# Layer 0's last group of the down product by seven products, its quarters folded as they finish

## The chip, the cores and the metric

One core of one Trainium2 chip runs the whole program. The metric is the time of one execution on the device, in microseconds (us), median of several runs.

## What is computed

Two layers on x of 512 tokens by 1024 features, all in float32. The reference, cut to what matters here:

```python
for layer in range(2):
    h = rms_norm(x, g_mix[layer])
    x = x + (even_mixer if layer == 0 else odd_mixer)(h, ...)     # projections, attention, output product
    h = rms_norm(x, g_mlp[layer])
    x = x + squared_relu_mlp(h, w_up[layer], w_down[layer])

def squared_relu_mlp(h, w_up, w_down):
    u = einsum("bsd,df->bsf", h, w_up)                  # 512 x 1024 by 1024 x 4096
    return einsum("bsf,fd->bsd", square(relu(u)), w_down)   # 512 x 4096 by 4096 x 1024
```

`rms_norm` divides a token's row by the root of its mean square and multiplies it by a gain per feature.

## The kernel before

Every float32 product is made of three products of a rounded high part and the low rest (`whi`, `wlo` of a weight; likewise of the data): high by high, low by high, high by low, added in one PSUM bank. A weight arrives by DMA as `wraw` or `mraw`; ScalarE (ACT) or GpSimd (POOL) copies the high part, VectorE (DVE) or POOL subtracts it for the low one. TensorE is PE in the profile, the DMA queue SP.

The function `mlp` makes a layer's second half out of a list of items. An item ("U", u) makes 256 of the 4096 hidden features in four steps of twelve matmuls (`up`). A down group collects four U items, 1024 hidden features. Three of layer 0's groups, and all four of layer 1's, are items ("T", g): a block scheme in which seven products take the place of eight. The table `ORDER` lists the seven (which weights, which data, which bank pair X, Y or Z), 28 steps of six matmuls; `combine_t` adds a finished bank, scaled per token by `r2col`, to one of four quarters `rest[e, t]` (feature half e, token half t). Sums of weight blocks are made on DVE by `sums_t`. With product 2 the scheme starts two banks of Y by one small product each (`L990`).

The last group of layer 0 is different: four items ("E", 3, dp), 16 steps of twelve matmuls (`direct`), each dp giving 256 features in the transposed layout that the next layer wants. For it the data of the U items 12 to 15 are scaled beforehand by a broadcast of the tokens' mean squares (`ssum`, the product of `L826`). The three T groups' quarters are turned by `fold` (four transposes and an add per 128 features) into the residual `back`, which comes back from `xmid`, while U 14 runs. `direct_end` then finishes 128 features at a time: add, high part `hn` on ACT, low on DVE, square on ACT, sum of squares on DVE.

Layer 1 begins with `vf_c`: `project` of 272 columns (values and forget gates), eight weights of 128x272 (k = 0 to 7, a step of 128 features each), twelve matmuls per weight into `pj0` to `pj3` (a bank for 128 tokens each). After a few of them (`STATS`) the caller runs `stats()`: `token_sums` on PE (`pc`) and `col_stats` on DVE, a chain of small instructions from `msv` to `rcol`. Then `use` needs `rcol`: `fz` on DVE, the four transposes `pz` on PE, the values `v` on ACT and DVE. `qk_c(0)` follows, 512 columns, in the same four banks; its eight tiles are split by `PAT_ATT`, that is, highs on POOL, lows by turns on DVE and POOL.

The order of each engine's instructions is set when the program is built; the engines work through theirs in order. Steps are counted in `mlp`'s main loop: weights are split six steps ahead (`R`), loads are issued two steps before that (`LS`), and `at(n, f)` puts an extra piece of work behind step n.

## Time and profile before

| | us |
|---|---|
| median of 3 runs (1156.47 to 1157.99) | 1157.99 |
| the profiled execution | 1157.34 |
| its span, first to last instruction | 1155.2 |
| PE busy | 1140.4 (99%) |
| DVE busy | 862.1 (75%) |
| ACT busy | 649.2 (56%) |
| POOL busy | 197.5 (17%) |
| mean granted clock of PE | 0.998 |

The span is the part that the trace covers; the time of the same execution is 2.1 us longer. A row of the timeline has the start from the span's first instruction, the length, the engine, the line of the code and what is written and read; `x8` counts instructions that were merged. Matmul rows overlap, since they are pipelined: their spacing tells the pace, not their length.

### The profile page before, as it was taken

Reading aid. Unit: us, or ns where it says so; the run is one execution under the profiler, and the core shown is the slowest. Engines: PE = TensorE matmul, PEld = TensorE weight load, DVE = VectorE, ACT = ScalarE, POOL = GpSimd, SP = SyncE. Lnnn points to the kernel's source line nnn. Section 1 sums busy time; section 2 is a strip of 40 time slices with the busy share of each in tenths; the row PEclk is TensorE's granted clock in tenths of the full one; section 3 lists DMA queues with packets and bytes.
Section 4 is the critical chain, followed back from the end, with each engine's and each line's share of the span. In section 5 each row is a group of like instructions: output and inputs, shape, how many; then the busy total and the mean of one; then the engine's idle time right before and its main releaser. Section 6 shows DMA issues by size and latency. Waiting matters only on the chain.

```text
span 1155.2 us, 16365 instructions
## 1 busy us (share of the span) xinstructions
PE 1140.4 (99%) x5758; PEld 956.8 (83%) x5758; DVE 862.1 (75%) x1791; ACT 649.2 (56%) x1344; POOL 197.5 (17%) x292
## 2 busy tenths in 40 slices
PE   9999999999999999999999999999999999999998
PEld 7987887888888888888988888888888888888887
DVE  7878999967857858755647877878848759669586
ACT  7555867656656455444326675665656455465452
POOL 0445524100000000000345545432000000000000
PEclk9999999999999999999999999999999999999999
DMA  8432114530531630723543333344420722523403
GB/s 289 132 92 74 40 54 146 200 129 37 185 107 37 219 110 4 250 72 105 154 123 108 103 106 99 106 128 128 164 74 25 231 73 70 186 73 115 150 28 110
DMA packets 91329, 133.83 MB, mean 116 GB/s; under 512 B 6112, under 2 KB 54240, under 8 KB 91248
## 3 DMA queue, kind: packets, MB, share of 16 engines
q1 hardware_dynamic: 90208, 130.63, 35.5%
q10 hardware_dynamic: 1040, 2.16, 0.5%
q8 instruction: 45, 0.74, 0.3%
q14 instruction: 36, 0.29, 0.1%
HBM read 119.63 MB, written 6.32 MB: 109 GB/s over the span
## 4 chain that ended last, share of the span: by engine, by line
PE 86%; DVE 6%; DMA 2%; ACT 2%; issue 2%; POOL 1%; SPq 0%; DVEq 0%; POOLq 0%; ACTq 0%
PE up L166 10%; PE up L170 10%; PE up L169 10%; PE pj L235 4%; PE pj L237 4%; PE pj L236 4%; PE Y L999 3%; PE Y L998 3%; PE Y L996 3%; PE O L406 3%; PE PT L386 2%; PE Z L999 2%; PE X L998 2%; PE Z L998 2%; PE X L999 2%; PE X L996 2%
## 5 line engine op out<-in xcount | busy, mean ns | idle before, releaser
L166 PE MATMUL up<-xin,whi 128*128 128x512 f32 x512 | 200.8, 392 | 0.0
L794 ACT CAST whi<-wraw 128x512 fp32r<-128x512 f32 x228 | 139.3, 620 | 107.5 <-PE up L170 47.8
L170 PE MATMUL up<-xin,whi 128*128 128x512 f32 x512 | 199.4, 389 | 0.0
L169 PE MATMUL up<-xin,wlo 128*128 128x512 f32 x512 | 199.2, 389 | 0.0
L795 DVE TENSOR_TENSOR wlo<-wraw,whi 128x512 fp32r<-128x512 f32 x228 | 150.6, 686 | 61.2 <-ACT whi L794 60.6
L154 POOL TENSOR_SCALAR whi<-wraw 128x512 fp32r<-128x512 f32 x88 | 58.2, 663 | 462.3 <-PE pj L237 419.8
L170 PEld LDWEIGHTS up<-xin,whi 128*128 128x128 f32 x512 | 96.1, 188 | 20.1
L169 PEld LDWEIGHTS up<-xin,wlo 128*128 128x128 f32 x512 | 96.2, 188 | 19.8 <-issue 0.2
L166 PEld LDWEIGHTS up<-xin,whi 128*128 128x128 f32 x512 | 96.1, 188 | 19.8 <-issue 0.2
L794 ACT CAST whi<-mraw 128x512 fp32r<-128x512 f32 x112 | 68.0, 620 | 53.1 <-DVE mraw L894 22.5
L366 ACT ACTIVATE P<-P,negm 128x128 f32<-128x128 f32 (+5 forms) x128 | 69.4, 543 | 41.9 <-DVE negm L363 39.4
L943 ACT ACTIVATE u<-up 128x512 f32<-128x512 f32 x64 | 38.3, 599 | 91.8 <-PE up L170 91.8
L235 PE MATMUL pj<-whi,hn 128*128 128x512 f32 (+2 forms) x256 | 88.7, 346 | 0.0
L237 PE MATMUL pj<-whi,hn 128*128 128x512 f32 (+2 forms) x256 | 86.9, 339 | 0.0
L236 PE MATMUL pj<-wlo,hn 128*128 128x512 f32 (+2 forms) x256 | 86.8, 339 | 0.0
L795 DVE TENSOR_TENSOR wlo<-mraw,whi 128x512 fp32r<-128x512 f32 x112 | 74.5, 683 | 6.5 <-ACT whi L794 6.4
L815 DVE TENSOR_TENSOR t<-u 128x256 f32<-128x256 f32 x56 | 23.2, 423 | 68.1 <-ACT u L1076 66.2
L157 POOL TENSOR_TENSOR wlo<-wraw,whi 128x512 fp32r<-128x512 f32 x48 | 64.3, 1341 | 21.2 <-ACT whi L152 18.7
L996 PE MATMUL Y<-whi,t 128*128 128x512 f32 x168 | 65.4, 389 | 0.0
L998 PE MATMUL Y<-wlo,t 128*128 128x512 f32 x168 | 65.4, 389 | 0.0
L999 PE MATMUL Y<-whi,t 128*128 128x512 f32 x168 | 65.4, 389 | 0.0
L374 POOL TENSOR_SCALAR P<-P,rden 128x256 f32<-128x256 f32 (+2 forms) x96 | 48.5, 508 | 83.2 <-DVE rden L369 77.7
(213 smaller groups left out, 2788.4 us busy)
## 6 DMA issues: line engine op xcount, KB each, us to landing
wraw<-in_w_up SPq DMA_DIRECT2D x64, 512.0 KB, 4.5
wraw<-in_w_down SPq DMA_DIRECT2D x50, 512.0 KB, 4.1
mraw<-in_w_down SPq DMA_DIRECT2D x28, 512.0 KB, 4.8
wraw<-in_w_in_odd SPq DMA_DIRECT2D x22, 512.0 KB, 3.6
wraw<-in_w_in_even SPq DMA_DIRECT2D x17, 512.0 KB, 4.9
K<-K SPq DMA_DIRECT2D x26, 256.0 KB, 2.9
bias<-csp SPq DMA_DIRECT2D x16, 256.0 KB, 3.3
wraw<-in_w_out_odd SPq DMA_DIRECT2D x8, 512.0 KB, 3.6
```

Of the source, the lines that this page charges most:

```text
L166: m = nc.tensor.matmul(o, wh, xh, start=start, stop=False, skip_group_check=more)
L169: nc.tensor.matmul(o, wl, xh, start=False, stop=False, skip_group_check=more)
L170: nc.tensor.matmul(o, wh, xl, start=False, stop=stop, skip_group_check=more)
L235: nc.tensor.matmul(o, xh, hi[:, :n], start=k == 0, stop=False)
L236: nc.tensor.matmul(o, xh, lo[:, :n], start=False, stop=False)
L237: nc.tensor.matmul(o, xl, hi[:, :n], start=False, stop=k == DC - 1)
L366: nc.scalar.activation(p[:, :ne], p[:, :ne], AF.Exp, scale=-1.0, bias=negm[:, i:i + 1], accum_out=den[:, i:i + 1])
L794: sca(nc.scalar.copy(dst_h, src))
L795: late.append(lambda: vec(nc.vector.tensor_sub(dst_l, src, dst_h.bitcast(F32))))
L996: m = nc.tensor.matmul(o, sh, hi, start=new and k == 0, stop=False, skip_group_check=not new)
L998: nc.tensor.matmul(o, sh, lo, start=False, stop=False, skip_group_check=not new)
L999: nc.tensor.matmul(o, sl, hi, start=False, stop=k == 3, skip_group_check=not new)
```

## The change

Layer 0's last group becomes an item ("T", 3) as in layer 1, right behind U 15. So `direct`, `direct_end`, the data scaled beforehand and the broadcast product go. The order of the seven products changes for all eight T groups: 12 is fourth, 4 sixth (before 4 fourth, 12 sixth), and weight block 12 is loaded four steps earlier. A quarter of `rest` is folded after the product that finishes it, in halves of 256 features by 256 tokens: (0, 0) behind steps 18 and 19 of the 28, (1, 1) behind 22 and 23, (0, 1) behind 26 and 27, (1, 0) after the last. Each fold takes four transposes, one add, two highs on ACT, two lows on DVE, a square on ACT and, from the second on, a sum of squares (POOL; DVE for the last quarter). `token_sums` adds two columns of partial sums, eight products for four. `back` returns into other buffers. `qk_c(0)` is split by ACT and DVE.

```diff
-FIN12 = (0, 5)
-BACK = (0, 0, 1, 1)
-FOLD = (0, 0, 1, 1, 2, 2, 3, 3)
-STATS = 3
+BACK = (2, 2, 7, 7)
+FOLD = {(0, 0): (18, 19), (1, 1): (22, 23), (0, 1): (26, 27), (1, 0): (28, 28)}
+STATS = 5
...
-                    return project([(g * 768, g * 768 + 512)], qk_use(g, 8))
+                    return project([(g * 768, g * 768 + 512)], qk_use(g, 8), PAT_ATT if g else PAT_START)
...
         for t in range(NT):
-            m = nc.tensor.matmul(pc[:, t:t + 1], ssum[:, t * P:(t + 1) * P], ones[:, :1], start=True, stop=True)
...
+            for k, a in enumerate(parts_):
+                m = nc.tensor.matmul(pc[:, t:t + 1], a[:, t * P:(t + 1) * P], ones[:, :1], start=k == 0,
+                                     stop=k == len(parts_) - 1)
...
-                pr = bank("pB", "r2")
-                tc.keep_in_program_order(nc.tensor.matmul(pr, ones, ssum, start=True, stop=True))
-                vec(nc.vector.tensor_scalar(ssum, pr, 1.0 / D, EPS, op0=OP.mult, op1=OP.add))
...
-                if g < 3 or last:
-                    items.append(("T", g))
-                else:
-                    items += [("E", g, dp) for dp in range(4)]
+                items.append(("T", g))
...
-            LOADS = {-2: 11, -1: 21, 0: 22, 6: 12, 16: 220}
+            LOADS = {-2: 11, -1: 21, 0: 22, 2: 12, 16: 220}
...
-            ORDER = ((11, "b11", "X"), (1, "t1", "Z"), (2, "t2", "Y"), (4, "b22", "Z"), (3, "t3", "Y"), (12, "b21", "X"),
+            ORDER = ((11, "b11", "X"), (1, "t1", "Z"), (2, "t2", "Y"), (12, "b21", "X"), (3, "t3", "Y"), (4, "b22", "Z"),
                      (22, "t4", "Y"))
...
-            def direct(j, p, hi, lo):
...
-            def direct_end(j, p):
...
-            def fold(c):
-
+            def fold(e, t, half):
+
+
+                dp = 2 * e + half
...
                 pt = bank("pB", "rT")
...
+                for cc in range(2):
+                    for b in range(2):
+                        pin("p", nc.tensor.transpose(pt[:, cc * 256 + b * P:cc * 256 + (b + 1) * P],
+                                                     rest[e, t][:, b, (2 * half + cc) * P:(2 * half + cc + 1) * P], ident))
+                ts = slice(t * 256, t * 256 + 256)
+                a = back[dp][:, :, ts]
+                vec(nc.vector.tensor_add(a, pt.rearrange("p (c t) -> p c t", c=2), a))
+                for cc in range(2):
+                    h, c = hn[2 * dp + cc], 2 * dp + cc
+                    g = gcol[:, 8 * (li + 1) + c:8 * (li + 1) + c + 1]
+                    sca(nc.scalar.activation(h[:, 0, ts], a[:, cc], AF.Copy, scale=g))
+                    late.append(lambda h=h, g=g, x=a[:, cc]: vec(nc.vector.scalar_tensor_tensor(
+                        h[:, 1, ts], x, g, h[:, 0, ts].bitcast(F32), op0=OP.mult, op1=OP.subtract)))
+                ss = res["ss"][:, :, ts]
...
+                    sq = mp.tile([P, 2, 256], F32, tag="sq", bufs=2, name="sq")
+                    sca(nc.scalar.activation(sq, a, AF.Square))
+                    if (e, t) == (1, 0):
+                        late.append(lambda: vec(nc.vector.tensor_add(ss, ss, sq)))
+                    else:
+                        pool(nc.gpsimd.tensor_add(ss, ss, sq))
+                if (e, t) in ((0, 1), (1, 0)):
+                    nc.scalar.dma_start(xsp[dp], back[dp])
...
-            return hn, lambda: col_stats(token_sums(res["ssum2"]))
+            return hn, lambda: col_stats(token_sums([res["ss"][:, k] for k in range(2)]))
```

What this does to the order of the instructions is seen best at layer 1's first projection. On DVE before, around the statistics (`msv`, `ecol`, `rsqb`, `rsq`, up to `rcol`); `wlo` of 128x272 is the low part of a weight of the first projection, of 128x512 one of the second:

```order
L967 SCALAR_TENSOR_TENSOR hn<-back,gcol,hn 128x512
L615 TENSOR_TENSOR ssum_5510<-ssum_5510,sqx 128x512
L157 TENSOR_TENSOR wlo<-wraw,whi 128x272
L141 TENSOR_SCALAR msv<-pc 128x4
L142 TENSOR_SCALAR ecol<-msv 128x4
L131 TENSOR_SCALAR rsqb<-msv 128x4
L132 TENSOR_SCALAR rsq<-rsqb 128x4
L157 TENSOR_TENSOR wlo<-wraw,whi 128x512
L134 SCALAR_TENSOR_TENSOR rsq<-msv,rsq 128x4
L759 MEMSET one 16x512
L135 TENSOR_TENSOR rsq<-rsq 128x4
L136 SCALAR_TENSOR_TENSOR rsq<-rsq 128x4
```

The eighth 128x272 low is the last instruction ahead of the statistics. On DVE in the changed program, from the same instruction on:

```order
L140 TENSOR_SCALAR msv<-pc 128x4
L141 TENSOR_SCALAR ecol<-msv 128x4
L130 TENSOR_SCALAR rsqb<-msv 128x4
L131 TENSOR_SCALAR rsq<-rsqb 128x4
L133 SCALAR_TENSOR_TENSOR rsq<-msv,rsq 128x4
L134 TENSOR_TENSOR rsq<-rsq 128x4
L135 SCALAR_TENSOR_TENSOR rsq<-rsq 128x4
L156 TENSOR_TENSOR wlo<-wraw,whi 128x272
L133 SCALAR_TENSOR_TENSOR rsq<-msv,rsq 128x4
L156 TENSOR_TENSOR wlo<-wraw,whi 128x272
L134 TENSOR_TENSOR rsq<-rsq 128x4
L156 TENSOR_TENSOR wlo<-wraw,whi 128x512
```

Two 128x272 lows now come behind seven and eight instructions of the statistics, and one 128x512 low less far behind them. The rows that follow there, to `rcol` and `fz`:

```order
L135 SCALAR_TENSOR_TENSOR rsq<-rsq 128x4
L760 MEMSET one 16x512
L133 SCALAR_TENSOR_TENSOR rsq<-msv,rsq 128x4
L156 TENSOR_TENSOR wlo<-wraw,whi 128x512
L134 TENSOR_TENSOR rsq<-rsq 128x4
L156 TENSOR_TENSOR wlo<-wraw,whi 128x512
L135 SCALAR_TENSOR_TENSOR rcol<-rsq 128x4
L156 TENSOR_TENSOR wlo<-wraw,whi 128x512
L746 SCALAR_TENSOR_TENSOR fz<-pj_5857,rcol,bfor 128x16
L746 SCALAR_TENSOR_TENSOR fz<-pj_5858,rcol,bfor 128x16
```

Between the last 128x272 low and `fz` stand four 128x512 lows, where before two stood in the whole chain. On PE in the changed program, around `pc` (`whi_5938` and `wlo_5939` belong to the sixth weight, `5995` and `5996` to the seventh, `5999` and `6000` to the eighth):

```order
L234 MATMUL pj3_5860<-whi_5938,hn_5732 128x272
L235 MATMUL pj3_5860<-wlo_5939,hn_5732 128x272
L621 MATMUL pc_5954<-ones_79,ss_5665 128x1 x8
L236 MATMUL pj3_5860<-whi_5938,hn_5732 128x272
L234 MATMUL pj0_5857<-whi_5995,hn_5750 128x272
L234 MATMUL pj1_5858<-whi_5995,hn_5750 128x272
L234 MATMUL pj2_5859<-whi_5995,hn_5750 128x272
L234 MATMUL pj3_5860<-whi_5995,hn_5750 128x272
L235 MATMUL pj0_5857<-wlo_5996,hn_5750 128x272
L236 MATMUL pj0_5857<-whi_5995,hn_5750 128x272
L234 MATMUL pj0_5857<-whi_5999,hn_5751 128x272
```

Before, `pc` stood behind the third weight's twelve matmuls, 36 of 96 in all; now it stands behind the sixth's but one, 71 of 96. On ACT in the changed program, from the last 128x272 highs to the values:

```order
L1044 DMA xsp<-back 128x1024
L151 CAST whi<-wraw 128x272 x2
L151 CAST whi<-wraw 128x512 x7
L160 ACTIVATE v_5853<-pj_5857,rcol 128x4x64
L160 ACTIVATE v_5853<-pj_5858,rcol 128x4x64
L753 ACTIVATE fe<-pz 16x512
```

Before, the last 128x272 high was followed at once by the four `v`; now seven 128x512 highs of the second projection stand between.

## Rows read from the trace of the kernel before

**Rows 1.** The page, part 1: busy us (share of the span) xinstructions.
```profile
PE 1140.4 (99%) x5758; PEld 956.8 (83%) x5758; DVE 862.1 (75%) x1791; ACT 649.2 (56%) x1344; POOL 197.5 (17%) x292
```

**Rows 2.** Timeline of PE, end of layer 0, layer 1's first projection: start, length, line, op.
```profile
519.85 0.39 PE L166 MATMUL dn<-s,whi 128*128 128x512 f32 x1
...
563.14 0.39 PE L170 MATMUL dn<-s,whi 128*128 128x512 f32 x1
...
563.37 0.28 PE L235 MATMUL pj<-whi,hn 128*128 128x272 f32 x1
...
567.88 0.95 PE L621 MATMUL pc<-ones,ssum 128*128 128x1 f32 x8
...
568.69 0.37 PE L235 MATMUL pj<-whi,hn 128*128 128x272 f32 x1
...
576.29 0.49 PE L749 MATMUL pz<-ident,fz 128*16 128x128 f32 x3
```

**Rows 3.** Timeline of DVE, same stretch: start, length, line, op, [idle before].
```profile
550.61 0.79 DVE L157 TENSOR_TENSOR wlo<-wraw,whi 128x272 fp32r<-128x272 f32 x2
...
568.86 0.16 DVE L141 TENSOR_SCALAR msv<-pc 128x4 f32<-128x4 f32 x1 [2.10 <-PE pc L621]
...
571.19 0.16 DVE L134 SCALAR_TENSOR_TENSOR rsq<-msv,rsq 128x4 f32<-128x4 f32 x1
...
571.39 1.15 DVE L135 TENSOR_TENSOR rsq<-rsq 128x4 f32<-128x4 f32 x1
...
574.68 0.53 DVE L745 SCALAR_TENSOR_TENSOR fz<-pj,rcol,bfor 128x16 f32<-128x16 f32 x2
...
575.45 0.48 DVE L162 SCALAR_TENSOR_TENSOR v<-pj,rcol,v 128x256 fp32r<-128x256 f32 x1 [0.23 <-ACT v L161]
```

**Rows 4.** Timeline of PE, last group of layer 1: the start-up products and the next matmul.
```profile
1115.45 0.61 PE L990 MATMUL Y<-whi,b 128*128 128x512 f32 x2
1115.90 0.39 PE L996 MATMUL X<-whi,b 128*128 128x512 f32 x1
```

**Rows 5.** Timeline of PE, mean squares of layer 0, then of layer 1.
```profile
254.70 0.95 PE L621 MATMUL pc<-ones,ssum 128*128 128x1 f32 x8
...
256.68 0.39 PE L169 MATMUL up<-xin,wlo 128*128 128x512 f32 x1
...
848.25 0.95 PE L621 MATMUL pc<-ones,ssum 128*128 128x1 f32 x8
...
849.38 0.39 PE L169 MATMUL up<-xin,wlo 128*128 128x512 f32 x1
```

**Rows 6.** Windows: length, busy PE PEld DVE ACT POOL, PEclk, DMA share, GB/s.
```profile
576.30:596.00 19.70, 19.70 (x91) 16.30 (x89) 6.24 (x12) 5.04 (x8) 10.87 (x12) 1.00 0.52 159
1112.70:1130.00 17.30, 17.30 (x78) 14.31 (x77) 15.95 (x24) 10.47 (x20) 0.00 (x0) 1.00 0.00 1
1130.00:1151.40 21.40, 21.40 (x95) 17.41 (x93) 15.39 (x24) 6.77 (x12) 0.00 (x0) 1.00 0.38 135
```

**Rows 7.** Groups of instructions by shape, 480 to 620 us: count, busy, mean ns, idle before.
```profile
L795 DVE TENSOR_TENSOR wlo<-wraw,whi 128x512 fp32r<-128x512 f32 x26 | 17.4, 686 | 6.2 <-ACT whi L794 6.1
...
L157 DVE TENSOR_TENSOR wlo<-wraw,whi 128x272 fp32r<-128x272 f32 x8 | 3.4, 436 | 0.7 <-ACT whi L152 0.7
...
L1029 DVE SCALAR_TENSOR_TENSOR rest<-Y,r2col,rest 128x512 f32<-128x512 f32 x2 | 1.4, 751 | 0.7 <-PE Y L999 0.7
...
L759 DVE MEMSET one<- 16x512 f32 x1 | 0.5, 485 | 0.0
```

**Rows 8.** The page, part 6, loads of layer 1's projection: KB each, us to landing.
```profile
wraw<-in_w_in_odd SPq DMA_DIRECT2D x22, 512.0 KB, 3.6
```

**Rows 9.** Timeline of POOL beside those DVE rows.
```profile
571.23 1.29 POOL L157 TENSOR_TENSOR wlo<-wraw,whi 128x512 fp32r<-128x512 f32 x1
```

**Rows 10.** Windows in layer 0, columns as above: PE busy, then PEclk.
```profile
99.80:103.56 3.76, 2.06 (x10) 1.09 (x9) 2.29 (x3) 0.12 (x1) 3.53 (x3) 1.00 0.74 211
103.56:106.98 3.42, 3.42 (x12) 2.84 (x11) 2.02 (x3) 1.04 (x2) 1.31 (x2) 0.50 0.00 0
```

More of the change, by code (lines that the diff above doesn't have):

```diff
@@ L1076, in square @@
                         sca(nc.scalar.activation(v[:, e], v[:, e], AF.Square))
-                def whole(e):
-                    s = slot("s") if u < 15 else mp.tile([P, 2, 512], F32R, tag="t24", bufs=2, name="s")
-                    halves(s[:, 0], s[:, 1], v[:, e])
-                    store[u, e] = s
-                def part(e):
-                    sca(nc.scalar.activation(v[:, e], v[:, e], AF.Square))
-                    vec(nc.vector.tensor_mul(v[:, e], v[:, e], ssum))
-                    whole(e)
-                    if u == 15:
-                        catch_up()
-                if not last and u >= 12:
-                    return [lambda: part(0), lambda: part(1)]
                 def tsum():
@@ L1106, in t_part @@
                 def t_part(i):
-                    if i and u % 4 == 0 and u:
+                    if i and (u % 4 == 0 and u or u == 15 and not last):
                         s = mp.tile([P, 2, 512], F32R, tag="t24", bufs=2, name="t24")
@@ L1129, in plan @@
                 n0 = first[j + 1]
-                if not last and u >= 12:
-                    offs = FIN12 if u == 12 else (0, 1)
-                else:
-                    offs = FIN15 if u == 15 else FIND if u % 4 == 0 and u else FIN
+                offs = FIN15 if u == 15 else FIND if u % 4 == 0 and u else FIN
                 for i, f in enumerate(unit_end(j)):
@@ L1150, in mlp @@
                     at(LEAVE[dp], lambda dp=dp: leave(dp))
-                    at(first[16] + BACK[dp], lambda dp=dp: come_back(dp))
-                for c in range(DC):
-                    at(first[17] + FOLD[c], lambda c=c: fold(c))
-                for n in range(8):
-                    at(first[6] + n, lambda n=n: vec(nc.vector.reciprocal(ssum[:, n * 64:n * 64 + 64],
-                                                                         ssum[:, n * 64:n * 64 + 64])))
+                    at(first[-1] + BACK[dp], lambda dp=dp: come_back(dp))
+                for (e, t), n in FOLD.items():
+                    for half in range(2):
+                        at(first[-1] + n[half], lambda e=e, t=t, half=half: fold(e, t, half))
             def end(n):
@@ L1161, in end @@
                 j, p = pos[n]
-                {"U": up_end, "E": direct_end, "T": combine_t}[items[j][0]](j, p)
-                if not last and items[j] == ("U", 15):
-                    if p % 2:
-                        unit_end(j)[p // 2]()
-                elif n + 1 == NP or pos[n + 1][0] != j:
+                {"U": up_end, "T": combine_t}[items[j][0]](j, p)
+                if n + 1 == NP or pos[n + 1][0] != j:
                     plan(j)
@@ L1186, in mlp @@
                 hi, lo = ready.pop(n)
[L1187 removed]
+                {"U": up, "T": product_t}[items[j][0]](j, p, hi, lo)
                 end(n - 1)
```

60 lines of the change are left out of this document (18 added, 42 removed).

## The prediction

> **What bounds the kernel now.** I read the page first: TensorE (PE) is busy 1140.4 us of the span of 1155.2 us [rows 1]. That is a claim about the whole, so I went to the stage that the change rewrites. The timeline of PE there shows the last down group of layer 0 as 192 matmuls from 519.85 to 563.14 without a hole, then layer 1's first projection, the four token sums `pc`, more of the projection, and the transposes `pz` [rows 2]. From 519.85 to 563.37 it is 43.52 us, 0.2267 us for one matmul of 512 columns. So a matmul taken away here is 0.2267 us less, unless a wait appears that these rows don't have. Where such a wait could come from is the row of VectorE (DVE) work after `pc`: from `msv` at 568.86 to `fz` at 574.68 DVE works on the statistics of the tokens, 5.8 us, and PE never notices, because 60 of the 96 projection matmuls stand behind `pc`: (567.88 - 563.37) / 36 = 0.125 us each, 7.5 us of cover [rows 2, 3].
>
> **TensorE's own work.** (a) The group takes 168 matmuls in place of 192: 24 x 0.2267 = -5.44 us. (b) It gets the two start-up products of line 990; in the last layer they put 0.45 us between 1115.45 and the next matmul [rows 4]: +0.45. (c) The broadcast product of the mean squares goes. With it 1.98 us lie between `pc` and the second matmul behind it (254.70 to 256.68), without it, in layer 1, 1.13 (848.25 to 849.38) [rows 5]: -0.85. (d) `token_sums` now has eight products for four; the four cost 568.69 - 567.88 = 0.81 [rows 2]: +0.81. (e) The 32 transposes of the folds stay 32 and only move: 0. Together -5.03 us. The weight splits of layer 1's second projection go from GpSimd (POOL) to ScalarE (ACT), all 16 lows to DVE; in the 19.70 us of that stage DVE is busy 6.24 and ACT 5.04 [rows 6], and eight more lows at 0.61 and sixteen highs of that size fit: 0 for the splits themselves. What they stand in front of is another matter, below. The new order of the products and the earlier load of `12` move one product's weights by a few steps in six groups in which PE has no wait; I take 0, and up to 0.3 us for each layer if one comes up short.
>
> **Wait A, the lows behind the statistics.** In the new program `pc` comes after 71 of the 96 projection matmuls, so only 25 are left to cover the statistics: 3.1 us. And the lows of the last two weights (128x272) now stand on DVE behind the first seven statistics instructions, where before all eight stood ahead. `msv` starts 0.17 us after PE has resumed (568.69, 568.86) [rows 2, 3]. Small instructions that depend on each other start 0.20 apart (571.19, 571.39), seven make 1.4; the low itself is 0.44, and two in a row take 0.79, so neighbours overlap by 0.08 [rows 3, 7]. The operand is there 2.0 us after PE resumes, PE has five matmuls for it, 0.63: **a wait of 1.4 us**.
>
> **Wait B, the transposes behind the scale.** From there to the first `fz` DVE has six more small ones (1.2), the other low (0.36), four lows of 512 columns (0.61 each with the overlap, 2.44), the memset (0.41) and `fz` itself (0.27): 4.7 us [rows 3, 7]. PE has 20 matmuls, 2.5, and then stands at `pz` in its own order: **2.1 us**.
>
> **Wait C, the banks of the values.** The next projection takes the banks that `fz` and the values `v` are read from. Before, from `fz` at 574.68 to the end of the first `v` on DVE at 575.93 were 1.25 us [rows 3]; `pz` covers some 0.8 of it, which leaves at least 0.5. But ACT now has splits of later weights ahead of its `v`. The last of them waits for a load whose buffer is freed by the second low: 0.6 us into wait B's row of work, plus 3.6 for the load [rows 8], 0.7 for the split (by DVE's row of that size), and twice 0.48 for `v` on ACT and DVE give 5.8, against 5.2 at which PE is through with `pz`. Bounds 0.5 and 1.5; I take **1.1**, nearer to the upper, since the load meets three writes of `xsp` in the queues and the fourth `v` is late too.
>
> **The folds.** In layer 1's last group, which the new one resembles, DVE is busy 15.95 of 17.30 us in the first part and 15.39 of 21.40 in the second [rows 6]. Into the second go five folds, each an add (0.61) and two lows of 128x256 (0.40 each with the overlap, by the row of `v`): 7.0 us into 6.0 idle and what the transposes lengthen. It fits as a sum, not at each step: 0 to 1.4, and I take 0.2. After the last matmul of the group DVE has three adds, two `rest` steps of 0.67 [rows 7], six lows of 128x256, three of 128x272 and two sums of squares, 8.0 us in all, while PE has 64 projection matmuls (8.0) and a dozen transposes before `pc`. So the sum of squares is ready less than 1 us before `pc` asks for it; that is the cover, and it is thin. Four sums of squares go to POOL. While POOL took its 1.29 us at 571.23, the small instruction of DVE at 571.39 lasted 1.15 in place of some 0.16 [rows 3, 9]. One such hold in the chain behind the last product is 0 to 1.3 us; I take the half, 0.6.
> The Trainium skill (SBUF — State Buffer, Who interferes with whom) makes this a rule: a VectorE instruction with two SBUF inputs and a GpSimd instruction that reads SBUF exclude each other for the whole instruction. By that rule the term is the full 1.3 and the sum 0.7 us longer; the 1.15 us row agrees with it.
>
> **The sum.** -5.03 + 1.4 + 2.1 + 1.1 + 0.2 + 0.6 = +0.4 us. Against the profiled execution (1157.34 us, of which 1155.2 are span) that is 1157.7. The median of the runs shown, 1157.99, stands 0.65 above that execution, so I forecast **1158.4 us: no change that can be told**. What a measurement of this kernel can tell from no change is about 0.2%, 2.3 us. The saved matmuls are real; what lay hidden under the long tail of even steps has lost its cover. Its own range, by the bounds of C, the folds and POOL and with 0.16 for a small instruction in A and B, is 1156.5 to 1160.7.
>
> **Rival 1, the chain stays hidden (faster).** If the statistics run quicker than the rows (POOL no longer stands in their way, and small instructions that don't depend on each other start closer together), or PE reaches `pc` later than I think, A and B shrink. It decides at the point where DVE finishes `fz` before PE has done 25 matmuls, 3.1 us after `pc`. Then -5.03 plus half a microsecond of C and a little for the folds: 1153.0 to 1154.5. For it: all before was hidden. Against: the rows in front of `fz` sum to 2.0 + 4.7 = 6.7 us, and with 0.16 for each small one still to 6.2.
>
> **Rival 2, TensorE's clock falls (slower).** Waits B and C lie side by side with four small transposes between: 3.2 us with hardly any PE work. In layer 0, from 99.80 to 103.56, PE was busy 2.06 of 3.76 us, and then the granted clock was 0.50, the lower of its two levels (1.2 and 2.4 GHz), for 3.42 us [rows 10]. The new stretch is emptier than that one. If it falls there, half of 3.42, 1.7 us, is lost on top of the forecast: 1160.1. Against: it would follow one stretch alone, and whether it does may differ between executions.
> The Trainium skill (TensorE: Matmul & The Clock Gate, Part 1) says that "the default state is throttled, and activity releases the throttle". By that the fall is to be expected behind a stretch like this, and the time would be the 1160.1; the rows of layer 0 agree.
>
> **Rival 3, the tail of the folds binds (slower).** POOL holds DVE for its whole 1.29 us more than once, the sum of squares comes after PE stands at `pc`, and everything behind shifts: +1.5 to +2.5 on the forecast, 1160 to 1161. The thin cover speaks for it, the moderate load of DVE after the group against it.
>
> **Chances.** Forecast 0.50, rival 1 0.18, rival 2 0.20, rival 3 0.12. Below 1155.7 lies rival 1 and nothing else: 0.18. Above 1160.3 lie half of rival 2 (its other half stays just under), two thirds of rival 3 and a rest of the forecast with both: 0.23. Between: 0.59. The range for 8 in 10 goes from the upper half of rival 1, 1153.4, to rivals 2 and 3 together, 1161.4.
>
> **What would show it.** Right: `dn` gone and 168 matmuls in its place, 36.5 us with no hole before the last product; three holes of PE, at a low of the seventh weight, at `pz` and at the second projection's first matmul, of 1.4, 2.1 and 1.1 us, all released by DVE; `msv` the instruction on which DVE idles before them. Wrong: PE without a hole between `pc` and the second projection (rival 1), PEclk at 0.50 near there (rival 2), or a wait in front of `pc` itself (rival 3). A wait inside one of the other six groups would say that I priced the new order of products wrongly.

## The result, and the profile after

The changed kernel takes **1159.14 us** (median of 20 runs, 1158.29 to 1160.80) against 1157.60 (20 runs, 1156.47 to 1159.08) for the kernel before: a ratio of 1.0016, with a 95% interval from 1.0009 to 1.0023. That is 1.5 us: the interval lies above 1, so the change costs a little, but less than the 0.2% that I called what can be told. The forecast was 1158.4, from 1153.4 to 1161.4, "no change that can be told". The profiled execution of the changed kernel took 1159.82 us, with a span of 1158.0.

The page, part 1, of the changed kernel (busy us, share of the span, instructions), against [rows 1]:

```profile
PE 1136.8 (98%) x5742; PEld 952.3 (82%) x5742; DVE 881.2 (76%) x1829; ACT 665.3 (57%) x1382; POOL 193.3 (17%) x284
```

TensorE (PE) works 3.6 us less, and yet the span is 2.8 us longer. So the matmuls did go, and more than they were worth came back, for the most part as idle time. Where, the timeline of PE shows. First the kernel before: two rows that I use as marks, layer 0's first `up` matmul and the first 512-column matmul of layer 1's second projection (start, length, line, op).

```profile
224.78 0.39 PE L166 MATMUL up<-xin,whi 128*128 128x512 f32 x1
...
576.53 0.48 PE L235 MATMUL pj<-whi,hn 128*128 128x512 f32 x1
```

The same view of the changed kernel, from the same mark over the new down group to the second projection. In brackets is the idle time in front and what ended it.

```profile
225.13 0.39 PE L165 MATMUL up<-xin,whi 128*128 128x512 f32 x1
...
515.71 0.39 PE L956 MATMUL X<-whi,b 128*128 128x512 f32 x1
...
553.86 0.30 PE L1021 MATMUL rT<-ident,rest 128*128 128x128 f32 x1 [0.72 <-DVE rest L989]
...
564.48 0.39 PE L235 MATMUL pj<-wlo,hn 128*128 128x272 f32 x1 [0.70 <-DVE wlo L156]
...
568.83 1.84 PE L621 MATMUL pc<-ones,ss 128*128 128x1 f32 x16
...
572.75 0.60 PE L235 MATMUL pj<-wlo,hn 128*128 128x272 f32 x1 [1.35 <-DVE wlo L156]
...
576.72 0.77 PE L750 MATMUL pz<-ident,fz 128*16 128x128 f32 x4
578.71 0.47 PE L234 MATMUL pj<-whi,hn 128*128 128x512 f32 x1 [1.23 <-DVE v L161]
```

From mark to mark it is 353.58 us (578.71 - 225.13) where it was 351.75 (576.53 - 224.78): 1.83 us more. (What lies before the first mark differs by up to 2.6 us between executions of these kernels, so I compare from the mark on.) The four bracketed rows are holes that the kernel before does not have in [rows 2]. In their order I call the first two the holes ahead of the token sums `pc`, the third is wait A and the fourth wait C of the prediction. Counted from the start of the matmul ahead of each, less that matmul's own 0.125, they are 0.89, 0.87, 1.51 and 1.39 us long. And there is a fifth loss that is not a hole: PE's granted clock. Windows of the changed kernel, columns as in [rows 6]:

```profile
568.83:572.38 3.55, 2.58 (x23) 2.36 (x21) 1.18 (x8) 1.76 (x3) 0.00 (x0) 1.00 0.50 193
572.38:575.79 3.41, 3.04 (x13) 3.04 (x14) 3.36 (x13) 0.00 (x0) 0.00 (x0) 0.50 0.43 116
575.79:578.71 2.92, 1.70 (x13) 1.20 (x12) 2.46 (x8) 2.17 (x5) 0.00 (x0) 1.00 0.82 255
```

Behind a stretch in which PE worked 2.58 of 3.55 us, the clock was at the lower of its two levels (1.2 in place of 2.4 GHz) for 3.41 us. The 13 matmuls in it start 0.227 us apart in place of 0.125: 1.3 us lost. All together: 0.89 + 0.87 + 1.51 + 1.39 + 1.3 = 6.0 us. The 1.83 us of delay and the 4.6 us of saved work that a control below shows make 6.4, so these five are nearly all of it.

DVE in the same stretch, against [rows 3]:

```profile
547.24 1.92 DVE L1030 SCALAR_TENSOR_TENSOR hn<-back,gcol,hn 128x256 fp32r<-128x256 f32 x2
...
551.58 0.87 DVE L1030 SCALAR_TENSOR_TENSOR hn<-back,gcol,hn 128x256 fp32r<-128x256 f32 x2
...
560.94 1.93 DVE L1030 SCALAR_TENSOR_TENSOR hn<-back,gcol,hn 128x256 fp32r<-128x256 f32 x2
...
567.24 0.68 DVE L1040 TENSOR_TENSOR ss<-ss,sq 128x512 f32<-128x512 f32 x1
570.71 0.16 DVE L140 TENSOR_SCALAR msv<-pc 128x4 f32<-128x4 f32 x1 [2.79 <-PE pc L621]
...
572.26 0.44 DVE L156 TENSOR_TENSOR wlo<-wraw,whi 128x272 fp32r<-128x272 f32 x1 [0.31 <-ACT whi L151]
572.62 0.15 DVE L133 SCALAR_TENSOR_TENSOR rsq<-msv,rsq 128x4 f32<-128x4 f32 x1
572.69 0.43 DVE L156 TENSOR_TENSOR wlo<-wraw,whi 128x272 fp32r<-128x272 f32 x1
...
576.29 0.86 DVE L746 SCALAR_TENSOR_TENSOR fz<-pj,rcol,bfor 128x16 f32<-128x16 f32 x4
```

And GpSimd (POOL) beside two of these rows:

```profile
546.95 1.53 POOL L1042 TENSOR_TENSOR ss<-ss,sq 128x512 f32<-128x512 f32 x1 [329.43 <-ACT sq L1038]
...
561.32 1.28 POOL L1042 TENSOR_TENSOR ss<-ss,sq 128x512 f32<-128x512 f32 x1 [1.62 <-ACT sq L1038]
```

Two things are to be seen. A pair of lows takes 0.87 us alone and 1.92 beside a sum of squares on POOL; I call this a hold, and it happens three times (the third is at 554.29, 1.90). And the low that PE waits for at 572.75 stands behind seven statistics instructions, after DVE had idled 2.79 us in front of `msv`. DVE also idles 0.31 us right in front of this low. The row puts that down to ACT, but in e5_fill, e2_pattern_back and f2_own_banks the same idle time has no releaser ("issue"), and in e1_squares_dve and g3_all_pool it is missing; its cause is open.

### The profile page after: what moved, and what is told of

Read it like the earlier page. It is cut to its first block, busy times and chain, and to the rows that moved or that the text cites. A ratio compares the mean times of both kernels' runs of the same rounds, so it can differ in the third digit from the quotient of the medians.

```text
span 1158.0 us, 16429 instructions
## 1 busy us (share of the span) xinstructions
PE 1136.8 (98%) x5742; PEld 952.3 (82%) x5742; DVE 881.2 (76%) x1829; ACT 665.3 (57%) x1382; POOL 193.3 (17%) x284
## 4 chain that ended last, share of the span: by engine, by line
PE 83%; DVE 8%; DMA 3%; ACT 2%; issue 2%; POOL 1%; SPq 0%; POOLq 0%; ACTq 0%; DVEq 0%
PE up L169 10%; PE up L165 10%; PE up L168 10%; PE pj L236 4%; PE pj L235 4%; PE pj L234 4%; PE Y L956 4%; PE Y L959 4%; PE Y L958 4%; PE O L405 3%; PE X L956 3%; PE X L959 3%; PE X L958 3%; PE Z L958 2%; PE Z L959 2%; PE Z L956 2%
## 5 line engine op out<-in xcount | busy, mean ns | idle before, releaser
L796 DVE TENSOR_TENSOR wlo<-wraw,whi 128x512 fp32r<-128x512 f32 x224 | 148.1, 687 | 65.4 <-ACT whi L795 64.8
L795 ACT CAST whi<-mraw 128x512 fp32r<-128x512 f32 x128 | 77.6, 619 | 62.8 <-PE X L959 18.4
L796 DVE TENSOR_TENSOR wlo<-mraw,whi 128x512 fp32r<-128x512 f32 x128 | 85.2, 684 | 9.6 <-ACT whi L795 9.5
L816 DVE TENSOR_TENSOR t<-u 128x256 f32<-128x256 f32 x64 | 26.4, 423 | 75.1 <-ACT u L1066 73.0
L153 POOL TENSOR_SCALAR whi<-wraw 128x512 fp32r<-128x512 f32 x80 | 54.9, 688 | 131.5 <-PE pj L236 107.4
L956 PE MATMUL Y<-whi,t 128*128 128x512 f32 x192 | 75.0, 390 | 0.0
L959 PE MATMUL Y<-whi,t 128*128 128x512 f32 x192 | 74.7, 389 | 0.0
L958 PE MATMUL Y<-wlo,t 128*128 128x512 f32 x192 | 74.7, 389 | 0.0
L156 DVE TENSOR_TENSOR wlo<-wraw,whi 128x512 fp32r<-128x512 f32 (+1 forms) x75 | 51.5, 694 | 18.3 <-POOL whi L153 15.0
L1042 POOL TENSOR_TENSOR ss<-ss,sq 128x512 f32<-128x512 f32 x4 | 5.4, 1354 | 339.7 <-ACT sq L1038 339.7
```

What stands on the lines that cost most here:

```text
L795: sca(nc.scalar.copy(dst_h, src))
L796: late.append(lambda: vec(nc.vector.tensor_sub(dst_l, src, dst_h.bitcast(F32))))
L956: m = nc.tensor.matmul(o, sh, hi, start=new and k == 0, stop=False, skip_group_check=not new)
L958: nc.tensor.matmul(o, sh, lo, start=False, stop=False, skip_group_check=not new)
L959: nc.tensor.matmul(o, sl, hi, start=False, stop=k == 3, skip_group_check=not new)
```

## The experiments

All ratios are to the kernel before, run beside it on the same chip. The mark is the distance between the two matmuls above, in the one execution of each kernel that was profiled, so it can differ from what the median does. It does not see what happens behind the second projection's first matmul. There a fall of the clock can still cost (f1_lows_first, g3_all_pool), and in the last six kernels of the table, from f2_own_banks on, the second projection is 0.22 to 0.30 us longer than the 32.89 us of the kernel before, since the `pz` transposes now lie in it.

| run | ratio, 95% interval | mark, us |
|---|---|---|
| kernel before | 1 | 351.75 |
| changed kernel | 1.0016 [1.0009, 1.0023] | 353.58 |
| e5_fill | 1.0018 [1.0010, 1.0027] | 353.33 |
| f1_lows_first | 1.0019 [1.0010, 1.0028] | 353.26 |
| e1_squares_dve | 1.0004 [0.9995, 1.0013] | 351.83 |
| g3_all_pool | 1.0017 [1.0008, 1.0027] | 353.70 |
| e2_pattern_back | 1.0027 [1.0016, 1.0038] | 354.40 |
| e4_order_back | 1.0021 [1.0012, 1.0030] | 353.59 |
| f2_own_banks | 0.9995 [0.9987, 1.0004] | 350.27 |
| f3_all | 0.9957 [0.9944, 0.9971] | 346.94 |
| f4_all_order | 0.9955 [0.9943, 0.9968] | 346.93 |
| g1_before_banks | 1.0009 [1.0001, 1.0018] | 351.51 |
| g4_pool_sums | 0.9972 [0.9960, 0.9984] | 348.63 |
| g2_all_pattern | 1.0005 [0.9993, 1.0016] | 350.12 |

**The theory.** VectorE's row of work from `msv` to `fz` and the values `v` decides when the second projection can start; what PE loses on the way there (a hole, a low clock) is only another form of that one wait. **The rivals:** each hole, and the fall of the clock, counts by itself; or the new order of the products, or the moved splits, cost the time.

### e5_fill: work for TensorE in the hole

```diff
                 stats()
+                fill = bank("pB", "fill")
+                for _ in range(7):
+                    tc.keep_in_program_order(nc.tensor.matmul(fill, hT[0][:, 0, :P], hT[0][:, 1], start=True, stop=True))
                 all_of(g)
```

> Seven matmuls of 512 columns on data that is there, into a bank that nobody reads, right behind the token sums, so that TensorE works through the wait for the lows of the seventh weight (7 x 0.227 = 1.6 us, the hole was 1.51). Theory (VectorE's chain sets the end; the fall of the clock lies inside the wait that would else stand before the pz transposes): the granted clock stays at 1.00 there, a hole of 1.0 to 2.0 us appears before pz, the second projection starts where it did within 0.3 us, and the time is 1159.1 within 0.4. Rival (the fall of the clock is paid in full): without it the second projection starts 1.7 us earlier and the time is 1157.4. Should the clock fall all the same, this run tells neither.

Measured: 1.0018, mark 353.33. Windows of this run, and then PE's rows at `pz` and the second projection:

```profile
567.73:571.65 3.92, 3.81 (x28) 3.30 (x26) 1.56 (x10) 1.34 (x3) 0.00 (x0) 1.00 0.45 175
571.65:574.80 3.15, 3.15 (x23) 2.98 (x23) 3.11 (x12) 0.71 (x2) 0.00 (x0) 1.00 0.51 137
574.80:577.37 2.57, 0.75 (x6) 0.38 (x5) 2.25 (x8) 1.98 (x5) 0.00 (x0) 1.00 0.90 276
```

```profile
575.46 0.70 PE L753 MATMUL pz<-ident,fz 128*16 128x128 f32 x4 [0.61 <-DVE fz L749]
577.37 0.47 PE L234 MATMUL pj<-whi,hn 128*128 128x512 f32 x1 [1.21 <-DVE v L161]
```

The clock stays at 1.00 and the hole behind the token sums is full of work, and nothing is won: a new hole stands before `pz`, released by `fz`, somewhat shorter than expected, and the second projection starts 0.25 us earlier. In the changed kernel's profiled execution the fall of the clock lies inside the wait for `fz`. It is not an extra loss. Its other runs agree: in two of the 20 the mean granted clock was 1.000, too high for a fall of 3.41 us (the profiled one has 0.999), and they took 1158.56 and 1159.14 us, where the median of all is 1159.14.

### f1_lows_first: the two lows ahead of the statistics

```diff
-                for _ in range(STATS):
+                for i in range(8):
+                    cnt["start"] = i == 6
                     next(g)
-                stats()
+                    if i == STATS + 1:
+                        stats()
+                cnt["start"] = False
                 all_of(g)
```

While `cnt["start"]` is set, the splits and statistics that are issued keep the order of the program.

> The changed kernel with the splits of the last two weights of layer 1's first projection, and the statistics, held in program order on VectorE, so that both lows stand ahead of msv, as they did in the kernel before. The changed kernel is 1.5 us above the kernel before. Theory (VectorE's row from msv to fz and the values sets when the second projection starts): the hole of 1.51 us behind the token sums is gone, the hole moves to the pz transposes, the second projection starts no earlier than in the changed kernel (353.6 us after layer 0's first up matmul) and up to 1.5 later, as the held statistics now have lows of 512 columns between them; 1 to 3 us above the kernel before. Rival (each hole counts by itself): 1.5 us less than the changed kernel, equal to the kernel before.

Measured: 1.0019, mark 353.26. PE, then DVE, in this run:

```profile
576.32 1.01 PE L753 MATMUL pz<-ident,fz 128*16 128x128 f32 x4 [3.44 <-DVE fz L749]
577.35 0.77 PE L234 MATMUL pj<-whi,hn 128*128 128x512 f32 x1
```

```profile
569.81 0.16 DVE L140 TENSOR_SCALAR msv<-pc 128x4 f32<-128x4 f32 x1 [2.22 <-PE pc L624]
569.89 0.69 DVE L156 TENSOR_TENSOR wlo<-wraw,whi 128x512 fp32r<-128x512 f32 x1
...
575.94 0.66 DVE L749 SCALAR_TENSOR_TENSOR fz<-pj,rcol,bfor 128x16 f32<-128x16 f32 x4
```

Wait A is gone, and one hole before `pz` takes its place: 3.60 us, counted as above, 3.44 of it idle. From `msv` to `fz` it is now 6.13 us where it was 5.58, since lows of 512 columns stand between the held statistics. The mark is 0.3 us earlier and not later: `v` on DVE follows `fz` without those lows between, and wait C has no row. But here the clock fell from 575.90 to 579.32, over the mark, and the second projection takes 33.66 us for 32.89, so the first scores (the matmul behind it) come 0.4 us later than in the changed kernel. The time is what the theory said. Taking one hole away gives nothing while the chain behind it is as long.

### e1_squares_dve and g3_all_pool: who adds the squares

```diff
-                    if (e, t) == (1, 0):
-                        late.append(lambda: vec(nc.vector.tensor_add(ss, ss, sq)))
-                    else:
-                        pool(nc.gpsimd.tensor_add(ss, ss, sq))
+                    late.append(lambda: vec(nc.vector.tensor_add(ss, ss, sq)))
```

> All eight sums of squares of the folds on VectorE; GpSimd does none. Changed kernel: 1159.14 us. Theory (GpSimd's sum holds a VectorE low for its whole time): the three pairs of lows of 1.9 us become 0.9, which gives 3.1 us of VectorE back, while four sums of 0.61 cost 2.4; the two holes of TensorE before the token sums (0.89 and 0.87 us) shrink to 1.0 together or less, and the time falls by 0.5 to 1.2 us. Rival (VectorE is simply full there, nothing is held): four more sums make the holes longer, 0.3 to 1.0 us slower.

Measured: 1.0004, mark 351.83, 1.75 us earlier. DVE:

```profile
546.20 0.88 DVE L1030 SCALAR_TENSOR_TENSOR hn<-back,gcol,hn 128x256 fp32r<-128x256 f32 x2
...
559.68 0.87 DVE L1030 SCALAR_TENSOR_TENSOR hn<-back,gcol,hn 128x256 fp32r<-128x256 f32 x2
```

Every pair of lows takes 0.87 to 0.89 us, and both holes ahead of the token sums are gone altogether, not only shorter: `pc` comes 1.56 us earlier from the first mark, and the other 0.19 are gained behind it. (There are six sums and not eight: two of the eight squares are the first of their token half and need none.) Four more sums on DVE cost less than three pairs of lows that POOL holds.

The other way round, with the last two sums on POOL too, so that `pool(nc.gpsimd.tensor_add(ss, ss, sq))` is the only branch:

> The changed kernel with the last two sums of squares on GpSimd too, six in place of four; the suspected cost is made larger. Theory (a GpSimd sum holds the VectorE low that meets it for its whole time, and the sums come in a row of 1.29 us each before the token sums): one or two more lows of 1.9 us, the token sums are waited for, and the time is 1 to 2.5 us above the changed kernel, that is 2.5 to 4 above the kernel before. Rival (the holes before the token sums came from VectorE's load): VectorE has 1.2 us less to do, 0 to 0.5 us below the changed kernel.

Measured: 1.0017, mark 353.70: a miss for both sides. DVE and POOL of this run:

```profile
565.96 2.98 DVE L156 TENSOR_TENSOR wlo<-wraw,whi 128x272 fp32r<-128x272 f32 x2
```

```profile
565.85 2.79 POOL L1039 TENSOR_TENSOR ss<-ss,sq 128x512 f32<-128x512 f32 x2 [2.43 <-ACT sq L1038]
```

The hold is there, two lows for 2.98 us that take 0.78 alone, and with it a third hole of PE ahead of the token sums (0.60 idle). The token sums come 0.65 us later, but the mark moves by 0.12 only: the wait at the lows of the seventh weight is shorter (0.85 idle for 1.35), for the most part because the 0.31 us of idle time in front of the first of them is missing; the row from `msv` to `fz` is 5.22 us for 5.58. In this execution the clock held behind wait A, and a hole stands before `pz` (0.99 idle); it fell from 579.12 to 582.53 instead, and the second projection takes 34.10 us for 32.89. The profiled execution, 1162.44 us, is the slowest of ten; their median is 1159.56. So the hold is shown and its price here is not what I took it for: by the ratio it is nothing, and why the 0.31 us are missing is open.

### e2_pattern_back: the splits back on GpSimd

```diff
-                    return project([(g * 768, g * 768 + 512)], qk_use(g, 8), PAT_ATT if g else PAT_START)
+                    return project([(g * 768, g * 768 + 512)], qk_use(g, 8))
```

> Only the splits of layer 1's second projection go back to GpSimd and VectorE as in the kernel before; all else as in the changed kernel (1159.14 us). Theory (VectorE's chain from msv to fz and the values sets when the second projection starts, and the lows of 512 columns stand in it): four of these lows at 0.61 us leave the chain, fz comes 2 us earlier (574.3 in place of 576.3), the hole before the second projection is under 0.5 us in place of 1.39, and the time is 1156.5 to 1157.5. Rival 1 (moving the splits cost nothing, as the prediction's sum has it): 1159 within 0.5. Rival 2 (GpSimd is too slow for a projection that starts without cover, its high and low take 1.9 us): holes inside the second projection, 1159 to 1161.

Measured: 1.0027, mark 354.40, 0.8 us later than the changed kernel: slower than the kernel before, and not faster than the changed kernel as the theory had it (the intervals of these two overlap). DVE, POOL and then windows of this run:

```profile
571.31 0.47 DVE L131 TENSOR_SCALAR rsq<-rsqb 128x4 int32<-128x4 int32 x1
...
576.72 0.23 DVE L746 SCALAR_TENSOR_TENSOR fz<-pj,rcol,bfor 128x16 f32<-128x16 f32 x1 [0.90 <-PE pj L236]
577.51 0.24 DVE L746 SCALAR_TENSOR_TENSOR fz<-pj,rcol,bfor 128x16 f32<-128x16 f32 x1 [0.56 <-PE pj L236]
```

POOL of this run beside the first of these rows:

```profile
570.42 1.33 POOL L153 TENSOR_SCALAR whi<-wraw 128x512 fp32r<-128x512 f32 x2
```

The windows:

```profile
569.00:573.30 4.30, 2.66 (x23) 2.44 (x23) 1.98 (x10) 0.00 (x0) 2.67 (x4) 1.00 0.17 66
573.30:576.71 3.41, 3.41 (x17) 3.41 (x17) 2.29 (x10) 0.84 (x2) 0.00 (x0) 0.53 0.60 181
```

`msv` to the first `fz` did get shorter: 575.35 - 570.84 = 4.5 us for 5.6. But GpSimd's splits now hold the lows ahead of the token sums (beside two highs and a low on POOL from 561.86 to 564.66, a low of 272 columns takes 0.76 us at 562.75 and a pair of lows 1.90 at 563.44). The token sums come 1.4 us later from the first mark, and with the chain short it is DVE that waits for PE, 0.90 and 0.56 us, while PE's clock is at its lower level. Here the fall of the clock is paid, where in the changed kernel it was free. The wait before the second projection itself is 0.20, as the theory had it.

### e4_order_back: the order of the products

```diff
+            if last:
+                ORDER = ORDER[:3] + (ORDER[5], ORDER[4], ORDER[3], ORDER[6])
-            LOADS = {-2: 11, -1: 21, 0: 22, 2: 12, 16: 220}
+            LOADS = {-2: 11, -1: 21, 0: 22, (6 if last else 2): 12, 16: 220}
```

> In layer 1 alone the products of the down groups go back to the order of the kernel before (4, 3, 12 in place of 12, 3, 4) and the load of quarter 12 to step 6; layer 0 stays as changed. Theory (the new order is free): the time stays within 0.3 us of 1159.14, and from layer 1's first up matmul to the last matmul the stretch is as long as in the changed kernel within 0.15 us. Rival (the new order or load costs what layer 1's MLP is longer than before): that stretch gets 0.37 us shorter, and the time 0.4 us.

Measured: 1.0021, which can't be told from the changed kernel. In the trace the stretch from layer 1's first `up` matmul to its last matmul is 0.36 us shorter, and all of it lies in the first down group. The first matmul of that group and of the `up` unit behind it, in the changed kernel and then in this run:

```profile
879.99 0.39 PE L956 MATMUL X<-whi,b 128*128 128x512 f32 x1
...
918.89 0.39 PE L165 MATMUL up<-xin,whi 128*128 128x512 f32 x1
```

```profile
877.86 0.39 PE L958 MATMUL X<-whi,b 128*128 128x512 f32 x1
...
916.39 0.39 PE L165 MATMUL up<-xin,whi 128*128 128x512 f32 x1
```

38.90 against 38.53 us. The other groups of both layers agree within 0.03. So the new order costs 0.37 us, once, in a place where PE waits for a low (0.45 us idle on its weight loads at 909.42). Why this group alone is open.

### f2_own_banks, f3_all, f4_all_order: the chain off the path

```diff
-                outs = [bank("pA", f"pj{t}") for t in range(NT)]
+                outs = [bank(banks, f"pj{t}") for t in range(NT)]
...
-                all_of(qk_c(0))
+                g = qk_c(0)
+                for _ in range(4):
+                    next(g)
+                forget(ap, st["z"])
+                all_of(g)
```

`qk_c(0)` passes "pB" for `banks`, all other projections "pA". `forget` is cut in two: `fz` stays where it was, and the `pz` transposes with what follows them stand in the second half, in a bank of "pA".

> The second projection of layer 1 gets its own four banks (those of tag pB), and the pz transposes come after a quarter of it, so TensorE needs neither fz nor the values to go on; all else as in the changed kernel. Theory (waits B and C are the wait for VectorE's chain, and A is a wait of its own): the holes at pz and before the second projection (1.39) are gone, A stays, and if the clock falls behind A the fall is now paid; the second projection starts 1.8 to 2.2 us earlier relative to layer 0's first up matmul (351.4 to 351.8 in place of 353.6), 0.5 to 0 us below the kernel before. Rival (the chain only moves: the weights' lows for the second projection, or the banks of the scores, come late): holes inside the second projection or before the first scores, no gain on the changed kernel.

Measured: 0.9995, mark 350.27, 3.3 us earlier than the changed kernel and thus more than expected. PE and windows:

```profile
572.01 0.39 PE L235 MATMUL pj<-wlo,hn 128*128 128x272 f32 x1 [1.34 <-DVE wlo L156]
...
574.64 0.40 PE L234 MATMUL pj<-whi,hn 128*128 128x512 f32 x1
```

```profile
568.09:572.00 3.91, 2.58 (x23) 2.35 (x21) 1.55 (x10) 1.75 (x3) 0.00 (x0) 1.00 0.45 176
572.01:574.64 2.63, 2.63 (x20) 2.63 (x21) 2.63 (x10) 0.18 (x1) 0.00 (x0) 1.00 0.41 106
```

B and C are gone, A is there as before, and the clock did not fall in this execution behind a stretch as thin as in the changed kernel. That, and `pz` behind the mark, is why the mark is earlier than the 351.4 to 351.8 that I expected with the fall paid. In other runs of this kernel the clock did fall somewhere: the four with a mean granted clock of 1.000 took 1155.48 to 1155.81 us, the seven below it 1156.33 to 1159.26. So the 3.3 us are those of an execution without a fall; by the two ratios, 0.9995 and 1.0016, the gain is 2.4.

With the two lows pinned ahead of `msv`, the token sums behind the whole first projection (`stats()` after all eight steps of `g`), and the sums of squares on VectorE:

> Three edits together: own banks and late pz as in f2_own_banks, the last two lows ahead of the statistics with the token sums behind the whole first projection, and all sums of squares on VectorE. Theory (the waits at the layer's junction eat the 5 us): no hole over 0.5 us from the end of the down group to the first scores' wait, no fall of the clock, the second projection starts 348.5 to 349.3 us after layer 0's first up matmul (353.6 in the changed kernel, 351.75 in the kernel before), and the time is 2.0 to 3.2 us below the kernel before. Rival (something else eats them, for instance loads of the second projection's weights): holes in the second projection, at most 1 us below the kernel before.

Measured: 0.9957, 1152.31 us against 1157.37, mark 346.94. PE has no bracketed row at all from 545 to 590 us. Two windows of PE that cover the end of the down group and the whole first projection:

```profile
549.00:556.00 7.00, 7.00 (x42) 6.08 (x41) 6.54 (x14) 3.93 (x10) 0.00 (x0) 1.00 0.43 115
556.00:570.96 14.96, 14.96 (x118) 14.47 (x117) 13.43 (x32) 9.31 (x22) 0.00 (x0) 1.00 0.75 250
```

Busy time equals the length of the window in both, at full clock. `fz` comes at 575.57, 7.5 us after `msv` where the changed kernel has 5.6, and nobody waits for it. The gain is 5.1 us, not the 2.0 to 3.2 expected: 353.58 less all five losses named above (6.0) is 347.6, and the expectation had not taken them all.

> As f3_all, and in layer 1 the products and the load in the order of the kernel before. e4_order_back showed 0.37 us for this in the first down group of layer 1; theory: 0.3 to 0.4 us less than f3_all, all of it in that group. Rival: that group's difference came from the data's place at that time, and nothing changes here.

Measured: 0.9955; the first down group of layer 1 is 0.34 us shorter (38.54 in place of 38.88), and the medians differ by 0.25 us. That agrees with the theory, but the times alone could not show it.

### g1, g4, g2: controls

> The kernel before with the own banks for layer 1's second projection and the late pz transposes; the down product, the place of the token sums and the splits stay as they were. Theory (f3_all is faster because the 5 us of matmuls that the change saves are no longer eaten; its extra edits give nothing by themselves where the statistics are hidden anyway): the second projection starts at most 0.3 us earlier than in the kernel before (351.45 to 351.75 us after layer 0's first up matmul), the ratio to it is 0.9993 to 1.0003. Rival (the own banks are a gain of their own, through the attention behind it): 1 us or more below the kernel before.

Measured: 1.0009 [1.0001, 1.0018], mark 351.51. From mark to mark the own banks give the kernel before 0.24 us, no more than the `pz` transposes that now lie behind the mark, and its time is no better, if anything 1 us worse (the attention behind it is 0.6 us longer in its trace). So f3_all is not fast because of the own banks and the late `pz` as such. Between g1_before_banks and f3_all lie 4.57 us from mark to mark: the saved matmuls, nearly whole.

> As f3_all, but with the four sums of squares on GpSimd as in the changed kernel. Theory (each term stands alone once VectorE's chain is off the path): the two holes of 0.9 us in front of the token sums are back, and the time is 1.5 to 1.9 us above f3_all, what e1_squares_dve took from the changed kernel. Rival (what is lost there is given back by the wait behind it): within 0.5 us of f3_all.

Measured: 0.9972, mark 348.63, 1.69 us later than f3_all, with the two bracketed rows (0.72 and 0.71 idle) back in their places. The price of the holds is about the same 1.7 us with the chain on the path and off it.

> As f3_all (5.0 us below the kernel before), with the splits of layer 1's second projection on GpSimd and VectorE in turn, as in the kernel before. Theory 1 (e2_pattern_back was slower because GpSimd's splits hold VectorE in the chain on which TensorE waited; with that chain off the path it doesn't matter): within 0.4 us of f3_all. Theory 2 (GpSimd's splits are too slow for this projection by themselves): holes inside the second projection, 1 to 2 us above f3_all.

Measured: 1.0005 [0.9993, 1.0016], mark 350.12, 3.2 us later than f3_all in the profiled execution. That one, 1155.45 us at a mean granted clock of 1.000, is the fastest of ten; their median is 1158.59, with clocks down to 0.994, and the ratios of g2_all_pattern and f3_all lie 0.0048 apart, 5.6 us. Where the clock fell in the other runs, no trace shows. Neither theory: the holes are not in the second projection, where theory 2 wanted them, but ahead of the token sums. DVE and POOL:

```profile
563.40 1.50 DVE L156 TENSOR_TENSOR wlo<-wraw,whi 128x272 fp32r<-128x272 f32 x1
...
565.85 1.51 DVE L156 TENSOR_TENSOR wlo<-wraw,whi 128x272 fp32r<-128x272 f32 x1
```

```profile
563.18 1.43 POOL L156 TENSOR_TENSOR wlo<-wraw,whi 128x512 fp32r<-128x512 f32 x1
...
565.61 1.45 POOL L156 TENSOR_TENSOR wlo<-wraw,whi 128x512 fp32r<-128x512 f32 x1
```

A low of 272 columns takes 1.50 us in place of 0.44 when GpSimd splits a weight of the *next* projection beside it, and PE waits 1.29 and 1.04 us for these two. The move of the splits off GpSimd, a part of the change that I had put at nothing, is worth 3.2 us at the mark with the chain off the path, and more in the median.

## Why the prediction was right, and where its steps were not

The class came out as forecast and the time lies 0.7 us above the forecast, inside the range. Against the kernel before, the forecast said +0.4 us and the runs say +1.5. The mechanism was right: TensorE's work went, and waits for DVE's row of work took its place. That the figure came so close is in part luck: wait B was priced 0.6 us or more too high and the holds 0.9 too low, and the two nearly cancel. Point by point:

- **TensorE's own work, -5.03.** Right within 0.5. With the waits taken away it shows: 4.57 us between g1_before_banks and f3_all (4.81 between the kernel before and f3_all, of which 0.24 are `pz` behind the mark). A part of what is missing is (e): the 32 transposes were put at no change, and they cost 3.80 us in f3_all, in smaller groups, for 3.53 in g1_before_banks (from the start of the matmul ahead to the second start behind, less the two matmuls' own). The 36.5 us up to the last product are worked out nowhere; the six products ahead of it take 34.88 (515.71 to 550.59), without a hole as forecast. Term by term, (c) is 0.89 in the trace (from layer 0's first `up` matmul to its first down product 55.30 us for 56.19) for 0.85 predicted, and (d) 0.89 (568.83 to 570.53 is 1.70, less 0.81) for 0.81.
- **Wait A, 1.4.** Right: the hole is 1.51, and the operand is a low behind seven statistics instructions, as the prediction put it. It holds 0.31 us of idle time of DVE that the working does not have.
- **Wait B, 2.1.** The wait was right and its form was not. In the profiled run PE never stands at `pz`, because it comes there late: the low clock's 1.3 us are in B's place. In e5_fill, where the clock holds, a hole is there. Its size was too large: in f1_lows_first A and B stand together as one hole of 3.60; less the 0.55 by which the chain is longer there, and less A's 1.51, that leaves 1.5 for B. The term that was mis-sized is the six small instructions: at 0.20 each they were to take 1.2 us, and in the changed kernel they move DVE's row on by 0.49 in all, four of them by 0.07, where a low follows (572.62, 572.69). From the end of the low (572.70) to that of the first `fz` (576.52) it is 3.8 us and not 4.7.
- **Wait C, 1.1.** Right within 0.3: the hole is 1.39, released by `v` on DVE.
- **The folds, 0.2, and POOL's holds, 0.6.** This is the step that failed. I priced one hold at half of 1.3 us "in the chain behind the last product" and looked for it at a small statistics instruction. The trace shows three holds of 1.03 to 1.06 us on pairs of lows, ahead of two holes of PE, and none in the statistics. Which of the three opens which hole was not tried by itself. e1_squares_dve and g4_pool_sums put the two terms together at 1.75 and 1.69 us for my 0.8. The full hold that the Trainium skill (SBUF — State Buffer, Who interferes with whom) gives for each meeting of a VectorE instruction with two SBUF inputs and a GpSimd instruction that reads SBUF was the better price, though my sentence counted one such meeting. The trace agrees with that rule in its numbers: 1.92 for 0.87, 2.98 for 0.78, 1.50 for 0.44.
- **The thin cover of the sum of squares, under 1 us.** Right: the last sum ends at 567.92, `pc` starts at 568.83.
- **The new order, 0 and up to 0.3 a layer.** 0.37 in layer 1, just above the bound that I gave, and nothing in layer 0.
- **The moved splits, 0.** Wrong: the move is a gain. Without it e2_pattern_back is 0.8 us later at the mark, and g2_all_pattern 3.2 later than f3_all.
- **Rival 1 (the chain stays hidden)** is refuted: A, C and the wait for `fz` are all there. One of its reasons was right, that small instructions start closer together than 0.20; it took some 0.7 us off B.
- **Rival 2 (the clock falls)** had its event and not its price. The clock fell for the 3.41 us that layer 0's rows showed, but behind wait A and not behind B and C. What I wrote, that half of it "is lost on top of the forecast", 1.7 us, is refuted for this place by e5_fill: PE lost in it what it would else have waited for. Over the second projection, where PE waits for nothing, a fall does cost (0.77 us in f1_lows_first, 1.21 in g3_all_pool). The Trainium skill (TensorE: Matmul & The Clock Gate, Part 1) made me expect the fall, and the changed kernel's windows agree; f2_own_banks, with the same 2.58 us of work around the same hole and no fall, shows that such a stretch does not bring it every time.
- **Rival 3 (the tail of the folds)** had the right mechanism, the holds, at another place: PE waits inside the first projection and never in front of `pc`.

The remainder lies behind the mark: from there to the last matmul the changed kernel's trace is 0.73 us longer, half of it the order, the other half in the attention. There the stretch from the first scores to layer 1's first `up` matmul is 208.90 us in the kernel before and 209.27 in the changed one, but 208.88 in e4_order_back and 209.51 in g1_before_banks, so 0.37 us is no more than these profiled executions differ by.

## What to carry to other kernels

A saved matmul is worth its time only as long as the chain that it used to hide stays hidden: count the cover behind the last reduction, before and after. When a chain sets the end, filling or removing one hole on the way gives nothing (e5_fill, f1_lows_first); let the waiting engine go on with work that needs none of the chain's results. Here other accumulation banks and a later transpose did that (f2_own_banks), and together with the lows ahead of the statistics, later token sums and all sums of squares on VectorE they turned 1.5 us lost into 5 us won (f3_all). And before GpSimd is given work "for free", look at which VectorE instructions run beside it and who waits for those.

## What the runs showed of the hardware that I had not expected

A hold does not need instructions of a like size, nor two inputs: a 128x4 statistics instruction that reads one tile took 0.47 us in place of 0.16, and ended with the two conversions that GpSimd had under way, in e2_pattern_back (571.31 beside 570.42). And a fall of TensorE's clock can be free where a wait stands behind it: the changed kernel with 3.41 us at 0.50, and e5_fill with none, start the second projection within 0.25 us of each other.
